# Layer 1's memory keys and values move into layer 0: projected during its attention, split into parts during its FFN

## The chip, the cores and the metric

The kernel runs on one core of a Trainium2 chip. The metric is device time in microseconds for one execution of the whole program. TensorE multiplies matrices into PSUM; VectorE and ScalarE work on SBUF and PSUM; GpSimd works on SBUF alone; the SyncE queue issues every load.

## The reference, cut to what matters

Two layers over 512 tokens of width 1024. Each layer normalises `x`, projects it, runs a token mixer on 12 heads (sparse attention with an index and a top-k in layer 0; compressed, selected and sliding-window attention in layer 1) beside a 4-head attention to a memory of 256 rows, projects all heads back and adds; then a SwiGLU FFN of width 2816 adds to `x`. The memory attention needs keys and values that depend on `mem`, on the layer's gain `mem_norm[i]` and on its weight alone, not on `x`:

```python
def memory_attention(q_mem, mem_n, w_kv_mem):          # mem_n = rmsnorm(mem, mem_norm[i])
    k, v = jnp.split(mem_n @ w_kv_mem, 2, axis=-1)     # 256 x 256 each
    s = jnp.einsum('bshd,bnhd->bhsn', q, k) * HEAD_DIM ** -0.5
    p = jax.nn.softmax(s, axis=-1)
    return jnp.einsum('bhsn,bnhd->bshd', p, v)
```

## The kernel before, in words

**Number format.** Every large product is made of three: an operand is cut into a high part of type fp32r and the rest, and `mm3` (lines 174 to 179) multiplies high by high, high by low and low by high. `weight` (line 159) loads a weight into one of four raw buffers (`wr`), ScalarE or VectorE casts the high part (`copy`, lines 148 and 150) and GpSimd or VectorE subtracts (lines 83 and 165). `raw` (line 168) loads into the same ring of four without cutting; it serves the memory projections, whose matmuls are plain fp32 and stand as two matmul instructions each in the trace.

**Stages.** `run` calls `setup`, `dsa` (layer 0's attention, 0 to 262 us of the profiled span), `ffn(0)` (to 610), `nsa` (layer 1's attention, to 916) and `ffn(1)`. An attention stage is a string of words, `SEQ[i]`, that `pipeline` turns into instructions in that order: `q:3` projects queries, `h:4` is the first half of a head unit (scores, exponentials, scaling of the rows), `H:4` the second (transposes on line 418, the cut of the weights on lines 422 to 427, weighted values on line 441), `m:0` and `M:0` the same for a pair of memory heads, `o:6` a part of the output projection, `t:128` so many steps of the top-k on VectorE (lines 686 to 692). The words give the priority; the framework's planner then writes a fixed order for each engine, in which an instruction may stand earlier than its word where the planner's own timeline has it ready.

**Memory.** `mem_stats` (word `ms`) makes the scale factors `mem_row` and `mem_col` once. `mem_kv(i)` (word `mkv`, in both strings) loads the memory again into four buffers of the tag `xs`, which also holds the 16 parts of the layer's normalised `x`, so that a buffer comes free when the last projection has read it. ScalarE multiplies eight pieces by the layer's gain (line 481); TensorE projects the keys (line 489), VectorE evicts them (line 491), and they are cut into a high and a low part, zero-padded by GpSimd (lines 494 to 498); TensorE projects the values (line 505) into two banks, and ScalarE and VectorE evict and cut them (lines 514 and 515). In layer 1 the word stands between `h:7` and `w:6`.

**PSUM.** Four tags share the eight banks: `mm`, `S` and `O` have two each, `T` four. Scores take `S` and `mm` in turn (`score_ps`).

Of the kernel before, what the change touches and what calls it, by code (L numbers as in the profile page):

```python
# [18 lines left out]
P = 128  # L19
# [10 lines left out]
OUT = -3e38  # L30
DOWN_SPLIT = (6, 5)
HALVED = 2
LAST = ("PPVP", "VVVV")
BUFS = {"xs": 17, "p": 10, "u": 8, "q": 12, "z": 2, "q1": 8, "qi": 4, "cy": 2, "k": 8, "m": 6, "r": 3, "t": 6, "o": 26, "o2": 6, "xg": 8}
RINGS = {"wr": 4, "wh": 3, "wl": 3}
STAY = {F32: 7 * KC + 2 + P + KC * S + S + P + NM + 1024 + 592 + RINGS["wr"] * KC * P, F32R: 4 * NB * P + 6 * P + (RINGS["wh"] + RINGS["wl"]) * KC * P}
BANKS = {"mm": 2, "S": 2, "T": 4, "O": 2}
FIRST = (0, 3)
IQ = False
# [6 lines left out]
CHUNKS = [((0, 1, 6, 7), (2, 3, 4, 5)), ((0, 1, 2), (6, 7, 3), (4, 5))]  # L46
TOPK = ((1, 2), (3,))
SEQ = ["""t:257 st iq:0 first iq:1 iq:2 iq:3 ix:1 ix:0 plan:1 ms ix:2 ix:3 kv mq:0 mq:1 q:2 q:0 q:3 t:128 h:4 q:1 h:0 q:4 q:5 mkv h:3 t:483 H:4 m:0
 m:1 h:1 h:5 M:0 M:1 h:2 H:3 h:6 t:5 H:2 h:9 H:6 H:5 H:9 h:8 h:7 H:0 plan:2 H:1 h:10 h:11 t:161 o:6 o:1 o:0 t:27 H:10 H:8 H:7 o:3 o:5 H:11
 o:7 o:4 o:2""",  # L50
       """plan:4 vc ks kc q:0 v ck kw h:0 plan:5 cv q:1 c:0 w:0 c:1 H:0 h:1 C:0 W:0 w:1 q:2 h:2 w:2 H:1 C:1 W:1 q:3 H:2 h:3 w:3 q:4 c:2 H:3 w:4 W:2
 w:5 W:3 C:2 h:4 c:3 q:5 h:5 H:5 mq:0 c:4 H:4 h:6 W:4 C:3 W:5 H:6 c:5 h:8 h:9 mq:1 h:7 mkv w:6 w:7 H:7 m:0 W:6 W:7 o:5 H:8 C:4 w:9 M:0 o:3
 o:2 m:1 o:1 h:10 o:0 H:9 o:6 W:9 w:8 w:10 M:1 o:7 o:4 W:8 C:5 h:11 H:10 o:12 o:11 w:11 H:11 W:10 o:13 W:11 o:9 o:14 o:8 o:10 o:15"""]
PLAN = [
    {"w": "V", "whi": "A", "stack": "P", "turn": "VP", "scale": "V", "shi": "A", "hhi": "VA", "hlo": "VP", "rmul": "VV", "radd": "V", "phi": "V", "plo": "V", "sqe": "PP", "irow": "VVPP", "sq": "PV"},
# [12 lines left out]
def r32(ap):  # L68
    return ap.bitcast(F32)
# [25 lines left out]
class Trunk:  # L95
# [378 lines left out]
    def mem_kv(self, i):  # L474
# [9 lines left out]
        for j in range(2):  # L484
# [12 lines left out]
                nc.scalar.copy(hi[h, sl], k[h])  # L497
                nc.vector.tensor_sub(lo[h, sl], k[h], r32(hi[h, sl]))
            keys.append((hi, lo))
        out = [self.ps(t)[:, :NM] for t in ("mm", "O")]  # L500
        for u in range(2):
            w = self.raw(io["wmv"][i, u])
            for b in range(2):
                for k in range(4):
                    nc.tensor.matmul(out[b], ms[4 * u + k][:, b * P : (b + 1) * P], w[:, k * NM : (k + 1) * NM], start=u + k == 0,
                                     stop=u == 1 and k == 3)
        vals = []
        for b in range(2):
            ps = out[b]
# [5 lines left out]
            nc.vector.scalar_tensor_tensor(dst[:, :, 64:], src, s, r32(dst[:, :, :64]), op0=ALU.mult, op1=ALU.subtract)  # L515
            vals.append(v)
        return keys, vals

    def mem_first(self, j, q, keys):

# [73 lines left out]
    def ffn(self, i):  # L594
        nc, io = self.nc, self.io
        xs, row = self.xs, None
        for half in range(2):
            acts = []
            for e in range(NFF // 2):
                j = half * (NFF // 2) + e  # L600
                g = self.proj(io["wf"][i, 2 * j], xs)
                u = self.proj(io["wf"][i, 2 * j + 1], xs, "S")
                if row is None:
                    row = self.stats()[1]
                a = self.slot("t", "fa")
                nc.vector.tensor_mul(a, g, row)  # L606
                nc.scalar.activation(a, a, AF.Silu)  # L607
                self.pool.tensor_mul(a, a, row)
                nc.vector.tensor_mul(a, a, u)  # L609
                hi, lo = self.pair("o", "f")  # L610
                nc.scalar.copy(hi, a)
                nc.vector.tensor_sub(lo, a, r32(hi))
                acts.append((hi, lo))
            for d in range(KC):
                if i and half and d == KC - HALVED:
                    self.down_last(acts)
                    break
                ps = self.ps("mm")
                k = 0
                for m in DOWN_SPLIT:  # L620
                    w = self.weight(io["wd"][i, half, d, :, k * P : (k + m) * P], m * P)
                    for e in range(m):
                        sl = slice(e * P, (e + 1) * P)
                        self.mm3(ps, (w[0][:, sl], w[1][:, sl]), acts[k], k == 0, k == NFF // 2 - 1)
                        k += 1
                nc.vector.tensor_add(self.x[d], self.x[d], ps)  # L626
                if half:
                    self.absorb(d, 1 if i == 0 else None)
                    if i:
                        self.last_gain(d, slice(0, S))  # L630
# [86 lines left out]
    def dsa(self):  # L717
# [75 lines left out]
        def query(j):  # L793
# [1 line left out]

        does = {"st": stats, "first": first, "iq": index_query, "ix": index, "ms": self.mem_stats, "kv": latent, "q": query,
                "mq": lambda j: self.mem_query(j, w, xs, row), "mkv": lambda: mkv.extend(self.mem_kv(0)), "t": self.tick,
                "o": lambda n: self.out_part(0, n % KC, CHUNKS[0][n // KC], "mm"), "plan": self.plan}
# [98 lines left out]
    def nsa(self):  # L897
# [31 lines left out]
        def comp_values():  # L929
# [2 lines left out]
        heads = [self.nsa_units(h, q, keys) for h in range(NH)]  # L932
        does = {"q": query, "mq": lambda j: self.mem_query(j, w, xs, row), "ks": lambda: key("ks"), "kw": lambda: key("kw"), "kc": lambda: unfold("kc"),
                "vc": lambda: unfold("vc"), "ck": comp_keys, "cv": comp_values, "v": lambda: self.values(col, xs),
                "mkv": lambda: mkv.extend(self.mem_kv(1)), "o": lambda n: self.out_part(1, n % KC, CHUNKS[1][n // KC], "mm"), "plan": self.plan}
# [232 lines left out]
```

## Time and profile before

| | |
|---|---|
| median of 3 runs | 1274.98 us (1273.6 to 1275.56) |
| the profiled execution | 1277.64 us, of which the span from first to last instruction is 1275.9 |
| TensorE matmul records, weight loads | 1234.9 us, 1026.0 us |
| VectorE, ScalarE, GpSimd | 622.1, 545.7, 798.4 us |
| mean granted TensorE clock | 0.980 of full |
| loaded from HBM | 105.25 MB |

A matmul's record is longer than the distance at which the next one can follow, so records overlap and a busy share near 100% may still hold idle time; the share of weight loads shows it better. Times of the trace are counted from the span's start. A row of the chain of waits says on which instruction, engine or transfer the last-ending chain of work stood, as a share of the stretch.

### The profile page before, as it was taken

The numbers are of one execution on the slowest core, as the hardware profiler recorded it, in microseconds if no ns is written. First come the engines' busy times: TensorE is split into PE (matmuls) and PEld (weight loads), VectorE is DVE, ScalarE is ACT, GpSimd is POOL, SyncE is SP. The second block draws the span as 40 slices with busy tenths as digits, with TensorE's granted clock in tenths as the row PEclk, the third lists the DMA queues.
The fourth block names the chain that finished last, engine by engine and source line by source line (L and its number), as shares of the span: only waits on it lengthen the run. The fifth ranks groups of instructions, "written<-read, shape, count | busy, mean of one in ns | idle before, by whom it ended". The sixth has DMA issues, their size and how long they took to land.

```text
span 1275.9 us, 17100 instructions
## 1 busy us (share of the span) xinstructions
PE 1234.9 (97%) x5882; PEld 1026.0 (80%) x5882; DVE 622.1 (49%) x1379; ACT 545.7 (43%) x1059; POOL 798.4 (63%) x1124
## 2 busy tenths in 40 slices
PE   7999889999999999999999999999999999999996
PEld 5888558888888888888888788887888888888886
DVE  6799976632221222234678998896521210111113
ACT  5535896433321223332247776785333322322231
POOL 9988884865543455447277674355986645667573
PEclk9999999999999999999986999999999999999998
DMA  7222002333223333223321101103232234333231
GB/s 267 89 74 89 11 1 76 99 99 99 89 78 100 118 95 99 81 89 116 107 99 50 36 15 57 32 32 118 78 96 96 85 88 114 111 97 91 69 91 66
DMA packets 40262, 108.44 MB, mean 85 GB/s; under 512 B 4720, under 2 KB 10480, under 8 KB 40176
## 3 DMA queue, kind: packets, MB, share of 16 engines
q1 hardware_dynamic: 40176, 107.36, 27.2%
q8 instruction: 46, 0.75, 0.3%
q14 instruction: 40, 0.33, 0.1%
HBM read 105.25 MB, written 2.10 MB: 84 GB/s over the span
## 4 chain that ended last, share of the span: by engine, by line
PE 77%; DVE 14%; ACT 3%; POOL 2%; DMA 2%; issue 1%; SPq 0%; DVEq 0%; ACTq 0%; POOLq 0%
PE ps L179 23%; PE ps L178 23%; PE ps L177 23%; PE ps L441 3%; PE ps L418 2%; DVE sc L690 2%; DVE stay L689 2%; DVE p L385 1%; DVE ul L427 1%; DMA mem<-in_memT 1%; POOL sq L83 1%; PE ps L380 1%; ACT p L391 1%; PE ps L381 1%; POOL stay L83 1%
## 5 line engine op out<-in xcount | busy, mean ns | idle before, releaser
L83 POOL TENSOR_TENSOR stay<-stay,stay 128x256 fp32r<-128x256 f32 (+1 forms) x601 | 441.5, 764 | 306.7 <-ACT stay L150 166.0
L150 ACT CAST stay<-stay 128x1024 fp32r<-128x1024 f32 (+4 forms) x208 | 189.4, 911 | 518.6 <-PE ps L178 455.3
L177 PE MATMUL ps<-xh,stay 128*128 128x512 f32 x912 | 358.9, 394 | 6.8 <-ACT xh L238 6.5
L179 PE MATMUL ps<-xh,stay 128*128 128x512 f32 x912 | 359.1, 394 | 1.2 <-DVE stay L165 1.2
L178 PE MATMUL ps<-xl,stay 128*128 128x512 f32 x912 | 358.0, 393 | 0.5 <-DVE xl L239 0.5
L177 PEld LDWEIGHTS ps<-xh,stay 128*128 128x128 f32 x912 | 173.4, 190 | 43.1 <-ACT xh L238 6.5
L179 PEld LDWEIGHTS ps<-xh,stay 128*128 128x128 f32 x912 | 173.0, 190 | 37.6 <-DVE stay L165 1.5
L178 PEld LDWEIGHTS ps<-xl,stay 128*128 128x128 f32 x912 | 172.9, 190 | 37.0 <-DVE xl L239 1.0
L178 PE MATMUL ps<-fl,stay 128*128 128x512 f32 (+1 forms) x352 | 134.8, 383 | 0.0
L179 PE MATMUL ps<-fh,stay 128*128 128x512 f32 (+1 forms) x352 | 134.6, 382 | 0.0
L177 PE MATMUL ps<-fh,stay 128*128 128x512 f32 (+1 forms) x352 | 134.6, 382 | 0.0
L609 DVE TENSOR_TENSOR fa<-fa,ps 128x512 f32<-128x512 f32 x44 | 30.2, 687 | 183.5 <-PE ps L179 166.1
L626 DVE TENSOR_TENSOR stay<-stay,ps 128x512 f32<-128x512 f32 x30 | 20.7, 689 | 155.6 <-PE ps L179 155.6
L606 DVE TENSOR_TENSOR fa<-ps,row 128x512 f32<-128x512 f32 x44 | 30.2, 690 | 128.2 <-PE ps L179 116.5
L391 ACT ACTIVATE p<-p,stay 128x384 f32<-128x384 f32 (+3 forms) x144 | 80.2, 559 | 18.0 <-DVE stay L385 17.4
L83 POOL TENSOR_TENSOR fa<-fa,row 128x256 f32<-128x256 f32 x88 | 65.3, 764 | 24.9 <-ACT fa L607 24.9
L177 PEld LDWEIGHTS ps<-fh,stay 128*128 128x128 f32 x352 | 66.1, 188 | 12.9
L178 PEld LDWEIGHTS ps<-fl,stay 128*128 128x128 f32 x352 | 66.1, 188 | 12.9
L179 PEld LDWEIGHTS ps<-fh,stay 128*128 128x128 f32 x352 | 66.2, 188 | 12.8
L83 POOL TENSOR_TENSOR p<-p,stay 128x128 f32<-128x128 f32 (+1 forms) x106 | 56.1, 557 | 32.4 <-DVE stay L401 21.7
L427 DVE TENSOR_TENSOR ul<-ps,uh 128x512 fp32r<-128x512 f32 (+1 forms) x103 | 62.7, 619 | 7.1 <-ACT uh L426 5.3
L418 PE MATMUL ps<-stay,p 128*128 128x128 f32 x360 | 55.8, 278 | 5.1 <-POOL p L83 2.1
(273 smaller groups left out, 2018.2 us busy)
## 6 DMA issues: line engine op xcount, KB each, us to landing
stay<-in_wf SPq DMA_DIRECT2D x88, 512.0 KB, 3.6
stay<-in_w SPq DMA_DIRECT2D x26, 512.0 KB, 3.5
stay<-in_wd SPq DMA_DIRECT2D x32, 384.0 KB, 3.1
stay<-in_wd SPq DMA_DIRECT2D x32, 320.0 KB, 2.9
mem<-in_memT SPq DMA_DIRECT2D x12, 256.0 KB, 3.8
stay<-in_wo SPq DMA_DIRECT2D x6, 512.0 KB, 3.5
stay<-in_wo SPq DMA_DIRECT2D x16, 192.0 KB, 2.4
stay<-in_xT SPq DMA_DIRECT2D x8, 256.0 KB, 6.7
```

The lines of the kernel that those rows point to most:

```text
L83: op(out[:, sl], x[:, sl], y[:, sl])
L150: self.nc.scalar.copy(out, x)
L177: mm(out, lhs[0], rhs[0], start=start, stop=False)
L178: mm(out, lhs[0], rhs[1], start=False, stop=False)
L179: mm(out, lhs[1], rhs[0], start=False, stop=stop)
L391: self.nc.scalar.activation(p, p, AF.Exp, scale=-1.0, bias=least, accum_out=total)
L418: nc.tensor.transpose(ps[:, off : off + P], ap, self.ident)
L427: nc.vector.tensor_sub(lo, ps[:, :w], r32(hi))
L441: self.nc.tensor.matmul(out, v if len(parts) > 1 else r32(v), t, start=start and i == 0, stop=stop and i == len(parts) - 1)
L606: nc.vector.tensor_mul(a, g, row)
L609: nc.vector.tensor_mul(a, a, u)
L689: nc.vector.max(m8, s)
```

## The change: what it does

`mem_kv` is no longer called for layer 1. Three new functions take its place. `next_keys(j)`, words `xk:0` and `xk:1` in layer 0's string, loads the memory (the first time), multiplies it by layer 1's gain, projects one of the two key tiles into a bank of tag `S` and evicts it, scaled, to a buffer of its own. `next_values`, word `xv`, projects both value tiles into one bank of tag `S` and evicts them through ScalarE. `next_parts` cuts the four tiles and is called in `ffn(0)` ahead of the second half. Four such buffers of 256 columns are added to the constant area. In `mem_kv`, which now serves layer 0 alone, the values go to the two halves of one `mm` bank, one output after the other, with both weights loaded ahead.

```diff
- ... h:1 h:5 M:0 M:1 h:2 H:3 h:6 t:5 H:2 h:9 H:6 H:5 H:9 h:8 ...            (SEQ[0])
+ ... h:1 h:5 M:0 M:1 xk:0 h:2 H:3 h:6 xk:1 t:5 H:2 h:9 H:6 H:5 xv H:9 h:8 ...
- ... h:8 h:9 mq:1 h:7 mkv w:6 w:7 H:7 m:0 ...                               (SEQ[1])
+ ... h:8 h:9 mq:1 h:7 w:6 w:7 H:7 m:0 ...
     def mem_kv(self, i):
...
-        out = [self.ps(t)[:, :NM] for t in ("mm", "O")]
-        for u in range(2):
-            w = self.raw(io["wmv"][i, u])
-            for b in range(2):
-                for k in range(4):
-                    nc.tensor.matmul(out[b], ms[4 * u + k][:, b * P : (b + 1) * P], w[:, k * NM : (k + 1) * NM], ...)
+        bank, ws = self.ps("mm"), [self.raw(io["wmv"][i, u]) for u in range(2)]
+        out = [bank[:, b * NM : (b + 1) * NM] for b in range(2)]
+        for b in range(2):
+            for k in range(KC):
+                nc.tensor.matmul(out[b], ms[k][:, b * P : (b + 1) * P], ws[k // 4][:, k % 4 * NM : (k % 4 + 1) * NM], ...)
+    def next_keys(self, j):
+        nc = self.nc
+        if j == 0:
+            self.next_mem, self.next_k, self.next_v = [], [self.c([P, NM], name="nk") ...], [self.c([P, NM], name="nv") ...]
+            for c, m in enumerate(self.load_mem("xs")):
+                for e in range(2):
+                    ...
+                    nc.scalar.activation(m[:, sl], m[:, sl], AF.Copy, scale=self.gains[:, g : g + 1])
+                    self.next_mem.append(m[:, sl])
+        ps, w = self.ps(NEXT[0])[:, :NM], self.raw(self.io["wmk"][1, j])          # NEXT = ("S", "S")
+        for k in range(KC):
+            nc.tensor.matmul(ps, w[:, k * P : (k + 1) * P], self.next_mem[k], start=k == 0, stop=k == KC - 1)
+        nc.vector.scalar_tensor_tensor(self.next_k[j], ps, -0.125, self.mem_row, op0=ALU.mult, op1=ALU.mult)
+    def next_values(self):
+        ... as the new lines of mem_kv, into self.ps(NEXT[1]), with layer 1's weights and self.next_mem
+        for b in range(2):
+            nc.scalar.activation(self.next_v[b], out[b], AF.Copy, scale=self.mem_col[:, b : b + 1])
+    def next_parts(self):
+        for k in self.next_k:
+            hi, lo = self.slot("m", "mkh", F32R), self.slot("m", "mkl", F32R)
+            for t in (hi, lo):
+                nc.gpsimd.memset(r32(t[:64, NM:]), 0.0)
+                nc.gpsimd.memset(r32(t[64:, :NM]), 0.0)
+            for h, sl in ((slice(0, 64), slice(0, NM)), (slice(64, P), slice(NM, S))):
+                nc.scalar.copy(hi[h, sl], k[h])
+                nc.vector.tensor_sub(lo[h, sl], k[h], r32(hi[h, sl]))
+        for v in self.next_v:
+            ...
+            nc.scalar.copy(dst[:, :, :64], src)
+            nc.vector.tensor_sub(dst[:, :, 64:], src, r32(dst[:, :, :64]))
     def ffn(self, i):
         for half in range(2):
+            if i == 0 and half == 1:
+                self.next_parts()
     def nsa(self):
-        mkv, z, keys = [], {}, {}
+        mkv, z, keys = self.next_kv, {}, {}
```

## Rows read from the trace of the kernel before

**Rows 1.** The page's engine line: busy us, share of the span, instructions.
```profile
PE 1234.9 (97%) x5882; PEld 1026.0 (80%) x5882; DVE 622.1 (49%) x1379; ACT 545.7 (43%) x1059; POOL 798.4 (63%) x1124
```

**Rows 2.** Layer 0's FFN, second half: the chain by line, then the busy-time window.
```profile
by line: PE ps L178 33.4%; PE ps L179 33.3%; PE ps L177 33.3%; PE ssq L201 0.1%
...
430.00:610.00 180.00, 180.00 (x798) 149.09 (x797) 55.42 (x68) 52.73 (x68) 94.42 (x125) 1.00 0.32 97
```

**Rows 3.** Windows, layer 1: busy PE, PEld, DVE, ACT, POOL; clock, DMA share, GB/s.
```profile
770.00:780.00 10.00, 10.00 (x60) 8.72 (x60) 9.88 (x34) 9.47 (x28) 2.87 (x4) 1.00 0.25 80
780.00:790.00 10.00, 10.00 (x49) 8.72 (x48) 7.45 (x17) 5.23 (x13) 7.44 (x12) 1.00 0.08 23
790.00:800.00 10.00, 10.00 (x56) 8.94 (x55) 6.26 (x22) 5.96 (x17) 3.51 (x6) 1.00 0.33 97
800.00:810.00 10.00, 9.44 (x53) 7.38 (x53) 8.44 (x22) 8.46 (x31) 1.86 (x4) 1.00 0.08 20
810.00:820.00 10.00, 9.42 (x59) 8.01 (x58) 9.94 (x23) 7.70 (x20) 3.23 (x6) 1.00 0.07 22
```

**Rows 4.** The chain of waits by line, 774 to 800 us.
```profile
by line: PE ps L489 26.8%; PE ps L505 16.7%; DMA stay<-in_wo 8.7%; PE ps L381 7.8%; PE ps L380 7.8%; PE ps L177 7.1%; PE ps L179 7.1%; PE ps L178 7.0%; PE ps L441 3.8%; DVE p L385 2.6%; ACT stay L150 2.0%; DVE mv L515 1.9%; ACT mv L514 1.5%
```

**Rows 5.** Windows as in rows 3, layer 0's attention; the last is solid TensorE.
```profile
130.00:150.00 20.00, 17.17 (x76) 11.55 (x75) 19.70 (x58) 14.89 (x56) 19.49 (x39) 0.91 0.05 14
150.00:165.00 15.00, 13.14 (x61) 8.39 (x58) 12.97 (x45) 14.76 (x41) 10.31 (x20) 1.00 0.00 0
165.00:180.00 15.00, 12.35 (x64) 8.32 (x65) 10.16 (x33) 13.80 (x36) 13.06 (x24) 1.00 0.01 2
180.00:195.00 15.00, 12.60 (x49) 8.79 (x48) 9.92 (x23) 11.32 (x29) 8.70 (x15) 0.89 0.00 1
...
210.00:236.00 26.00, 26.00 (x126) 21.64 (x125) 13.99 (x24) 13.36 (x23) 12.09 (x15) 1.00 0.31 102
```

**Rows 6.** The chain by line, 130 to 165 us and 165 to 195 us.
```profile
by line: DVE sc L690 17.0%; DVE stay L689 15.8%; DVE p L385 13.7%; DVE stay L528 12.9%; ACT p L391 11.8%; DVE ul L427 5.4%; issue 3.8%; DVE ho L450 3.7%; ACT ho L449 3.3%; ACT oh L150 3.2%; ACT uf L422 2.9%; DVE stay L397 2.6%; DVE ho L838 
...
by line: PE ps L441 26.6%; PE ps L418 15.7%; ACT ho L837 9.4%; ACT p L391 8.1%; ACT uh L426 5.8%; PE ps L177 4.4%; ACT p L411 4.4%; PE ps L380 4.1%; PE ps L381 4.1%; ACT uf L422 4.0%; ACT o L150 3.4%; PE ps L179 3.0%; PE ps L178 3.0%; issue
```

**Rows 7.** Matmuls that read the memory, 690 to 810: duration, first and last start.
```profile
L489 PE MATMUL ps<-mem,stay x32: 378/379/431, 782.1 to 791.2; 128*128 128x256 f32 x32
L505 PE MATMUL ps<-stay,mem x32: 377/379/382, 783.0 to 797.8; 128*128 128x256 f32 x32
```

**Rows 8.** Timeline of TensorE: a run of twenty.
```profile
787.12 4.48 PE L489 MATMUL ps<-mem,stay 128*128 128x256 f32 x20
```

**Rows 9.** Window 774 to 805, lines 498, 515, 491, 497, 514 in turn: busy, count.
```profile
774.00:805.00 31.00, 2.16 (x4) 1.00 0.24 71
...
774.00:805.00 31.00, 0.96 (x2) 1.00 0.24 71
...
774.00:805.00 31.00, 0.85 (x2) 1.00 0.24 71
...
774.00:805.00 31.00, 1.61 (x4) 1.00 0.24 71
...
774.00:805.00 31.00, 0.95 (x2) 1.00 0.24 71
```

**Rows 10.** Line 481: durations, its waits, a run; then one of the memsets.
```profile
L481 ACT ACTIVATE mem<-mem,stay x16: 492/496/512, 24.0 to 782.8; 128x256 f32<-128x256 f32 x16
...
  DMA mem<-in_memT: 3.5, 3
...
109.03 1.71 ACT L481 ACTIVATE mem<-mem,stay 128x256 f32<-128x256 f32 x4 [1.80 <-DMA mem<-in_memT]
...
L494 POOL MEMSET mkh<- x4: 303/304/304, 0.9 to 135.2; 64x256 f32 x4
```

**Rows 11.** The load queue: wo in layer 1; what it waited for, 130 to 260.
```profile
784.72 15.90 SPq L163 DMA_DIRECT2D stay<-in_wo  x7
...
SPq L163 <- ACT stay L150: 83.6, 8, 62.0
```

More of the change, by code (lines that the diff above doesn't have):

```diff
@@ L32 @@
 HALVED = 2
+NEXT = ("S", "S")
 LAST = ("PPVP", "VVVV")
@@ L35 @@
 RINGS = {"wr": 4, "wh": 3, "wl": 3}
[L36 removed]
+STAY = {F32: 7 * KC + 2 + P + KC * S + S + P + NM + 1024 + 592 + 4 * NM + RINGS["wr"] * KC * P, F32R: 4 * NB * P + 6 * P + (RINGS["wh"] + RINGS["wl"]) * KC * P}
 BANKS = {"mm": 2, "S": 2, "T": 4, "O": 2}
@@ L499, in mem_kv @@
             keys.append((hi, lo))
-        out = [self.ps(t)[:, :NM] for t in ("mm", "O")]
-        for u in range(2):
-            w = self.raw(io["wmv"][i, u])
-            for b in range(2):
-                for k in range(4):
-                    nc.tensor.matmul(out[b], ms[4 * u + k][:, b * P : (b + 1) * P], w[:, k * NM : (k + 1) * NM], start=u + k == 0,
-                                     stop=u == 1 and k == 3)
+        bank, ws = self.ps("mm"), [self.raw(io["wmv"][i, u]) for u in range(2)]
+        out = [bank[:, b * NM : (b + 1) * NM] for b in range(2)]
+        for b in range(2):
+            for k in range(KC):
+                nc.tensor.matmul(out[b], ms[k][:, b * P : (b + 1) * P], ws[k // 4][:, k % 4 * NM : (k % 4 + 1) * NM], start=k == 0, stop=k == KC - 1)
         vals = []
@@ L517, in mem_kv @@
         return keys, vals
+    def next_keys(self, j):
+        nc = self.nc
+        if j == 0:
+            self.next_mem, self.next_k, self.next_v = [], [self.c([P, NM], name="nk") for _ in range(2)], [self.c([P, NM], name="nv") for _ in range(2)]
+            for c, m in enumerate(self.load_mem("xs")):
+                for e in range(2):
+                    sl = slice(e * NM, (e + 1) * NM)
+                    g = 3 * KC + 2 * c + e
+                    nc.scalar.activation(m[:, sl], m[:, sl], AF.Copy, scale=self.gains[:, g : g + 1])
[4 more added lines that the diff above has]
+        nc.vector.scalar_tensor_tensor(self.next_k[j], ps, -0.125, self.mem_row, op0=ALU.mult, op1=ALU.mult)
@@ new lines, in next_values @@
+    def next_values(self):
+        nc = self.nc
+        bank, ws = self.ps(NEXT[1]), [self.raw(self.io["wmv"][1, u]) for u in range(2)]
+        out = [bank[:, b * NM : (b + 1) * NM] for b in range(2)]
+        for b in range(2):
+            for k in range(KC):
+                nc.tensor.matmul(out[b], self.next_mem[k][:, b * P : (b + 1) * P], ws[k // 4][:, k % 4 * NM : (k % 4 + 1) * NM], start=k == 0, stop=k == KC - 1)
+        for b in range(2):
+            nc.scalar.activation(self.next_v[b], out[b], AF.Copy, scale=self.mem_col[:, b : b + 1])
@@ new lines, in next_parts @@
+    def next_parts(self):
+        nc, keys, vals = self.nc, [], []
+        for k in self.next_k:
[6 more added lines that the diff above has]
+                nc.vector.tensor_sub(lo[h, sl], k[h], r32(hi[h, sl]))
+            keys.append((hi, lo))
+        for v in self.next_v:
+            t = self.slot("m", "mv", F32R)
+            src, dst = v.rearrange("p (h d) -> p h d", h=4), t.rearrange("p (h d) -> p h d", h=4)
+            nc.scalar.copy(dst[:, :, :64], src)
+            nc.vector.tensor_sub(dst[:, :, 64:], src, r32(dst[:, :, :64]))
+            vals.append(t)
+        self.next_kv = keys, vals
```

8 lines of the change are left out of this document (4 added, 4 removed).

## The prediction

> **What bounds the kernel now.** I read the page's engine line first: TensorE 97% busy, the other engines 43 to 63% [rows 1]. A busy record of TensorE is longer than the pitch at which its matmuls follow each other, so 97% hides idle time; I therefore go stage by stage, by ten-microsecond windows and by the chain of waits. Layer 0's FFN is TensorE alone: its chain is the three lines of the split product, a third each, while VectorE has 55.4 of 180 us to do and GpSimd 94.4 [rows 2]. The two attention stages are not like that, and the change lives in them.
>
> Layer 1, around the block that is taken out: the reader sees VectorE at 9.88 of 10 us just before it, at 7.45 and 6.26 in the two windows of 780 to 800, and at 8.44 and 9.94 after, while TensorE is full throughout [rows 3]. The chain of 774 to 800 names the cause: 43.5% of it is lines 489 and 505, the memory projections, and another 8.7% a wait for a weight of the output projection [rows 4]. So VectorE, else the bound there, starves for these 20 us while TensorE projects memory.
>
> Layer 0, 130 to 195 us: VectorE has 19.70 of 20 us to do until 150, ScalarE 14.76 of 15 and 13.80 of 15 until 180; weight loads, which take 21.64 of 26 us where TensorE is full, take 37.05 of these 65 [rows 5]. At the full stretch's share (0.832) these are 44.5 us of solid TensorE, so about 20.5 us of it are free, an estimate. The chain goes over VectorE's top-k lines and ScalarE's exponentials first and is 61% TensorE's from 165 to 195 (lines 441, 418, 177, 380, 381, 179, 178) [rows 6].
>
> **Layer 1: what goes.** 64 matmul instructions of 128x256 (32 on line 489, 32 on line 505) [rows 7]; twenty in a row take 4.48 us, so the pitch is (4.48 - 0.38) / 19 = 0.216 us [rows 8], and all take 13.8 us. VectorE loses 2.16 + 0.96 + 0.85 = 3.97 us, ScalarE 1.61 + 0.95 in the same stretch [rows 9] and eight scalings of 0.496 us each [rows 10]. What is left of 780 to 800 is 20 - 13.8 = 6.2 us on TensorE and 13.71 - 3.97 = 9.74 on VectorE; ScalarE's list is shorter than that, GpSimd's is as long but has idle time on both sides [rows 3]. So VectorE is late next. At the neighbours' mean load (9.88, 8.44 and 9.94 of 10, that is 0.942) its 9.74 us take 10.3, and the gain is 9.7 us. The ends: 4.0 us, if VectorE stays the bound without a break so that only its own share is won; and 14.5 us, the chain's part that the block causes (26 us times 0.435, 0.087 and the 0.034 of lines 514 and 515) [rows 4]. A loss there is excluded: every engine's list only gets shorter and the rest of the order string is unchanged. I take 9.7, since VectorE is the nearer limit in the rows.
>
> In the queue of the loads, two of wmv leave the ring of four raw buffers, so the seven loads of wo that now start only at 784.72 [rows 11] can come sooner; the 8.7% of the chain that waits for one, 2.26 us, belongs to the upper end, not to the 9.7.
>
> **Layer 0: what is added.** The same 64 matmuls, 13.8 us, against the 20.5 us free: I cost them at nothing; without that cover, at TensorE's 61% of the chain from 165 to 195, 13.8 x 0.61 = 8.4 us. ScalarE gets eight scalings, in a row 1.71 / 4 = 0.43 us each [rows 10], and two evictions of values at about 0.47 (half of line 514's 0.95): 4.3 us. It has 10.2 us idle from 130 to 195, 5.1 of them before 150 where VectorE is the bound, nearly none from 150 to 165 [rows 5]. The scalings need only the landed memory and can lie early, the evictions cannot: I cost half, 2.15 us (ends 0 and 4.3). VectorE gets two evictions of keys, half of 0.85 us each; half of that on the chain, 0.4 (ends 0 and 0.85). Sum 2.5 us.
>
> Below nothing: the granted clock is 0.91 of full in 130 to 150 and 0.89 in 180 to 195 [rows 5], so TensorE ran some 3.5 us at its lower level, 1.2 GHz, in each, after thin stretches. Matmuls that fill these could keep it at 2.4 GHz; in 180 to 195, where TensorE is on the chain, that gives back 15 x 0.11 = 1.65 us. The ends of layer 0 are thus -1.65 and 4.3 + 0.85 + 8.4 = 13.5. The Trainium skill, "TensorE: Matmul & The Clock Gate", section "What's actually happening", has the gate follow how busy TensorE has recently been; by it the sum would be better by those 1.65 us. I leave it in the range, since the rows do not show that the dips lie where the new matmuls fall.
>
> The loads are four of memory, two of wmk and two of wmv. They enter the queue ahead of the first wo loads and take the four raw buffers, so each of those wo loads waits until its predecessor's matmuls have read. In this stage the queue stood idle behind full buffers for up to 62.0 us at a time [rows 11]; I cost it at nothing, and at one landing like that one, 2.26 us, if the values' projection runs so late that the output projection at 190 has no weight.
>
> **FFN and the small edits.** The splitting put ahead of layer 0's second FFN half costs VectorE 2.16 + 0.96, ScalarE 1.61 + 0.95 and GpSimd eight memsets of 0.30 us [rows 9, 10]; the stage's chain is TensorE's alone and hides all of it [rows 2]. If that cover were gone it would be VectorE's 3.1 us. Layer 0's own values now go to one bank, output by output: same matmuls, and at worst its two evictions one after the other, 0.95 us; I take 0.
>
> **Sum.** -9.7 + 2.5 = -7.2 us. The profiled execution took 1277.64 us, which gives 1270.4; it lies 2.66 above the median of the runs, 1274.98, and against that the forecast is 1267.8 us.
>
> **Rivals.** *The moved matmuls meet a TensorE that is on the chain.* Place: layer 0 from 165 on. Its matmuls run in the order written at build time; if the projections of xk:1 and xv stand ahead of the heads' transposes and weighted products, they delay these by 8.4 us; if they slip behind 195, where TensorE is full, by the whole 13.8. With the 2.5 of the other engines that is 10.9 to 16.3 against a gain of 9.7: 1.2 to 6.6 slower, 1279 us in the middle. It decides from the point at which more than about half of the 13.8 us is on the chain (7.2 us). For it: the order string puts all three behind the memory heads, and 165 to 195 is 61% TensorE's. Against: in layer 1 the lines 489 and 505 lie interleaved rather than in one block (the second starts at 783.0, the first's last at 791.2) [rows 7], so such matmuls can fill holes, and 20.5 us are free. *VectorE does not let go.* Layer 1 gives only its 4.0 us, layer 0 takes 2.5: -1.5, or 1273.5 us. For it: 9.88 and 9.94 of 10 on either side; against: 6.3 us of idle VectorE inside the block. *Everything fits.* The chain's 14.5 us go, layer 0 takes 1: 1261.5 us. For it: the wo loads come sooner; against: VectorE's 9.74 us have to be done somewhere. *ScalarE waits at the head of its queue.* ScalarE stood idle 3.5 us in three waits of line 481 for the memory's landing [rows 10]; if the new scalings come to its head before their loads have landed, the exponentials behind them wait as long: -7.2 + 3.5 = -3.7, or 1271.3 us. Against: the loads can be issued long before 150, and only one of the waits shown is as long as 1.80. The Trainium skill, "TensorE: Matmul & The Clock Gate", section "Architectural detail", says that ScalarE's queue is strictly first in, first out; by that rule nothing overtakes the scalings, and the trace's waits agree.
>
> **Chances.** Forecast 0.52 (own range 1264 to 1271), everything fits 0.14, VectorE 0.16, ScalarE's queue 0.06, TensorE on the chain 0.12. A measurement of this kernel can tell about 0.2%, 2.5 us, from no change. Faster: the first two, most of ScalarE's queue (0.05) and a little of VectorE's (0.03): 0.74. The same: most of VectorE's and small parts of others, 0.13. Slower: the TensorE rival and the worse side of VectorE's, 0.13. The range 1261 to 1278 leaves out half of the two outer cases.
>
> **What would show it.** Right: in layer 1's attention no matmul of a memory projection, VectorE above 9 of 10 us through the former block, and the stage from 610 to 916 shorter by 8 to 11 us; in layer 0 the 64 matmuls between 125 and 195 with TensorE's weight loads up from 37 us and layer 0's FFN starting 1 to 4 us later; the FFN as long as before. Wrong: a later FFN start by more than 7 us, idle VectorE where the block was, or the projections behind 195.

## The result and the profile after

The changed kernel takes 1288.97 us (median of 4 runs, 1287.87 to 1290.33), the kernel before 1275.27 us beside it (1273.6 to 1276.11): a ratio of 1.0107, 95% interval 1.0095 to 1.0118. It is 13.7 us slower; 7.2 us faster was forecast.

The profiled execution's span is 1288.6 us against 1275.9. Cut where TensorE starts the first product of the next stage's input, the spans fall into these parts (us; read from the traces; these cuts lie earlier than the rough bounds of 262 and 916 us named ahead of the prediction; the kernels after the first two are experiments below):

```
                       layer 0's    layer 0's   layer 1's    layer 1's
                       attention    FFN         attention    FFN
before                   247.2        362.0       288.0        378.7
after                    263.7        361.9       284.7        378.2
l1_only                  244.1        362.0       280.2        378.7
l0_only                  253.6        362.0       290.8        378.4
first_key_on_gpsimd      256.9        361.9       280.7        378.4
before_3T                247.5        363.6       295.8        378.7
after_3T                 259.9        363.6       282.8        378.8
cut_in_ffn_3T            250.5        362.0       284.7        378.4
```

A row is one execution, and a part of it can differ by some 3 us without any edit: l1_only's layer 0 has the written order of before on TensorE, VectorE and ScalarE and is 3.1 us shorter. In its first 50 us TensorE had its full clock, in before it was granted 0.93, in the changed kernel 0.93 too, in *l0_only* and *first_key_on_gpsimd* 1.00.

So, at the same clock at the start, layer 0's attention took 16.5 us more than before, layer 1's 3.3 less, the FFNs the same. Line numbers are from here on those of the kernel that a row comes from; the changed kernel's are higher than before's by 1 up to line 500 and by 45 to 47 behind the new functions. First the engine line of the changed kernel, which answers to [rows 1], and its chain by line in the second half of layer 0's FFN with the window, which answer to [rows 2]:

```profile
PE 1240.3 (96%) x5882; PEld 1031.5 (80%) x5882; DVE 634.1 (49%) x1379; ACT 546.2 (42%) x1061; POOL 797.0 (62%) x1124
...
by line: PE ps L180 33.4%; PE ps L179 33.4%; PE ps L178 33.3%
...
446.00:626.00 180.00, 180.00 (x796) 149.06 (x795) 55.11 (x67) 53.17 (x68) 94.54 (x125) 1.00 0.32 97
```

VectorE has 12.0 us more to do over the whole span, for work that was only moved, and no more of it in the FFN (55.11 against 55.42), where the cut was to stand. The cut's four subtractions for the keys are line 554 (the two for the values, line 560, start at 185.9 and 186.5 us); the trace has them here (line, count, shortest/median/longest ns, first and last start), after them the projections:

```profile
L554 DVE TENSOR_TENSOR mkl<-stay,mkh x4: 422/1655/6294, 145.9 to 174.8; 64x256 fp32r<-64x256 f32 x4
...
L531 PE MATMUL ps<-mem,stay x32: 377/379/796, 138.9 to 170.0; 128*128 128x256 f32 x32
...
L540 PE MATMUL ps<-stay,mem x32: 378/379/382, 174.8 to 183.5; 128*128 128x256 f32 x32
```

All four stand in layer 0's attention, between 145.9 and 174.8 us: the cut hangs only on the projected tiles, and the planner drew it forward from the FFN, where the program's text has it, into the attention. One of the four took 6294 ns instead of the 0.54 us that such a subtraction took in layer 1 before (2.16 us for four) [rows 9]. The timelines of VectorE and of GpSimd around it:

```profile
145.92 6.29 DVE L554 TENSOR_TENSOR mkl<-stay,mkh 64x256 fp32r<-64x256 f32 x1 [0.66 <-ACT mkh L553]
152.14 0.68 DVE L736 MAX8 stay<-sc 128x8 f32<-128x512 f32 x1
```

```profile
145.57 0.72 POOL L81 TENSOR_TENSOR o<-ho,o 128x256 fp32r<-128x256 f32 x1
146.26 2.89 POOL L84 TENSOR_TENSOR mp<-mp,stay 128x256 f32<-128x256 f32 x5
149.11 1.40 POOL L84 TENSOR_TENSOR stay<-stay,stay 128x256 fp32r<-128x256 f32 x2
150.47 1.46 POOL L84 TENSOR_TENSOR p<-p,stay 128x128 f32<-128x128 f32 x4
```

GpSimd works without a gap; the 12 instructions shown run from 145.57 to 151.93. VectorE's subtraction, which reads two tiles in SBUF, starts 0.35 us into the first of them and ends at 152.21, just after the last is over. Behind it VectorE's pass over the scores (line 386) is late, ScalarE's exponentials (line 392) wait 5.9 us for that, and TensorE's transposes (line 419) as long. These are TensorE's two longest waits from 120 to 215 us (total, times, longest); the second ends at 204.7 and is another one, for a cast in ScalarE's queue:

```profile
PE ps L419 <- DVE stay L386: 5.9, 1, 5.9
PE ps L178 <- ACT o L151: 3.1, 1, 3.1
```

The windows of layer 0's attention (columns as in [rows 3]) answer to [rows 5]: in 150 to 165 TensorE is busy 9.88 of 15 us and was 13.14, ScalarE 7.83 and was 14.76, and TensorE's granted clock is 0.77 there, where it was full before; in 195 to 210 it is 0.78. TensorE so loses the wait, and then runs part of the stretch behind it at 1.2 GHz.

```profile
130.00:150.00 20.00, 16.30 (x71) 11.72 (x71) 18.47 (x41) 14.44 (x55) 15.10 (x30) 0.91 0.04 14
150.00:165.00 15.00, 9.88 (x39) 6.23 (x40) 12.85 (x37) 7.83 (x20) 6.53 (x13) 0.77 0.05 17
165.00:180.00 15.00, 15.00 (x77) 12.39 (x76) 14.00 (x35) 12.42 (x36) 10.67 (x20) 1.00 0.12 36
180.00:195.00 15.00, 15.00 (x75) 11.28 (x74) 9.42 (x26) 13.61 (x35) 8.70 (x15) 1.00 0.15 54
195.00:210.00 15.00, 11.44 (x44) 8.72 (x44) 9.97 (x27) 12.02 (x31) 10.93 (x21) 0.78 0.00 1
```

The chain by line, 120 to 215 us, answers to [rows 6]. VectorE's top-k (lines 736 and 737) has 4.3% and 3.1% of it, where it had 8.6% and 9.3% in the same stretch of before, and the two moved projections stand in it with 7.3% each, 13.9 of 95 us. Before, then after:

```profile
by line: PE ps L441 12.3%; PE ps L418 9.6%; DVE sc L690 9.3%; DVE stay L689 8.6%; ACT p L391 6.9%; DVE p L385 6.1%; PE ps L177 5.7%; PE ps L179 5.0%; PE ps L178 5.0%; DVE stay L528 4.7%; ACT ho L837 3.0%; ACT uf L422 2.3%; DVE mkl L498 2.2%
...
by line: PE ps L442 14.8%; PE ps L419 10.9%; issue 8.8%; PE ps L531 7.3%; PE ps L540 7.3%; ACT p L392 6.1%; DVE stay L736 4.3%; ACT mp L576 4.1%; DVE sc L737 3.1%; DVE p L386 2.8%; DVE mkl L499 2.7%; ACT ho L884 2.7%; DMA stay<-in_wo 2.7%; 
```

In layer 1, where the block was, VectorE is now busy 12.51 of 14 us (8.9 of 10), against 7.45 and 6.26 of 10 [rows 3], so that the idle VectorE is gone nearly as forecast (above 9 of 10):

```profile
783.00:797.00 14.00, 13.05 (x93) 11.69 (x92) 12.51 (x39) 11.63 (x33) 5.19 (x9) 1.00 0.00 1
```

### The profile page after: what moved, and what is told of

The parts are those of the page before. It is cut to its first block, busy times and chain, and to the rows that moved or that the text cites. A ratio compares the mean times of both kernels' runs of the same rounds, so it can differ in the third digit from the quotient of the medians.

```text
span 1288.6 us, 17111 instructions
## 1 busy us (share of the span) xinstructions
PE 1240.3 (96%) x5882; PEld 1031.5 (80%) x5882; DVE 634.1 (49%) x1379; ACT 546.2 (42%) x1061; POOL 797.0 (62%) x1124
## 4 chain that ended last, share of the span: by engine, by line
PE 77%; DVE 12%; POOL 4%; ACT 3%; issue 2%; DMA 1%; DVEq 0%; SPq 0%; ACTq 0%; POOLq 0%
PE ps L180 23%; PE ps L179 22%; PE ps L178 22%; PE ps L442 3%; PE ps L419 2%; POOL sq L84 2%; DVE sc L737 2%; DVE p L386 2%; DVE stay L736 1%; DVE ul L428 1%; POOL stay L84 1%; PE ps L381 1%; DVE p L410 1%; PE ps L382 1%; ACT p L392 1%
## 5 line engine op out<-in xcount | busy, mean ns | idle before, releaser
L427 ACT CAST uh<-ps 128x512 fp32r<-128x512 f32 (+1 forms) x103 | 53.2, 534 | 17.8 <-PE ps L419 14.9
```

The lines of the kernel that those rows point to most:

```text
L427: nc.scalar.copy(hi, ps[:, :w])
```

## The experiments

The order of every engine is written by the planner, so an edit moves other instructions too. Each experiment is therefore compared with the kernel that differs from it by the one edit; times are medians, ratios are to the kernel before with a 95% interval.

**The two halves apart.** *l1_only* is the kernel before without layer 1's memory keys and values (layer 1 uses layer 0's, so its output is another); *l0_only* is the changed kernel whose layer 1 makes its own again as before, the early ones being made and left unused.

```diff
- mkv, z, keys = [], {}, {}                  # l1_only; and "mkv" out of SEQ[1]
+ mkv, z, keys = self.first_kv, {}, {}       # what mem_kv(0) made
- ... mq:1 h:7 w:6 w:7 ...                   # l0_only
+ ... mq:1 h:7 mkv w:6 w:7 ...               # with mkv.extend(self.mem_kv(1))
```

> Before, with layer 1's memory projection and cut taken out and nothing put in its place: layer 1's memory heads read layer 0's keys and values (that part of the computation is left out). If the forecast's step for layer 1 is right, the time falls by about 9.7 us (1265.5). The changed kernel's layer 1 only gained 3.3 us, having lost 6 us between 700 and 777 before it won 9.2 at the former block. If that loss belongs to the removal, this run gains about 3 us (1272); if it belongs to what is added in layer 0, this run gains 9 to 10.

> The changed kernel, with layer 1 projecting and cutting its own memory as before, so that the work put into layer 0 is done and not used. If the two layers add up, layer 0's cost of 16.5 us stands alone: 1291 to 1292 us, and layer 1 is as long as before (288.0 us). If part of the cost came from layer 1's shorter string, it is less than 1289.

l1_only: 1267.38 us, 0.9945 [0.993, 0.996], 8.2 us faster than the 1275.53 beside it. l0_only: 1288.11 us, 1.0111 [1.0091, 1.0131], 12.6 slower than the same. The removal is worth nearly what was forecast; the loss is layer 0's. But the halves do not add up: 12.6 - 8.2 is 4.4 us slower, the whole change 13.7, and l0_only lies under the 1291 to 1292 expected of halves that do.

A piece is missing in l0_only. Its layer 0 has the changed kernel's written order (but for eight memsets on GpSimd), so the two profiled executions can be laid side by side. l0_only's (the fastest of its runs, 1286.59) spent 253.6 us there, not 263.7: none of its four subtractions took over 1.09 us, though the first also begins just behind the start of a GpSimd instruction. That subtraction and GpSimd beside it in l0_only, then the transposes of TensorE behind it in l0_only and in the changed kernel, then the first 50 us of both in that order:

```profile
143.34 0.69 DVE L554 TENSOR_TENSOR mkl<-stay,mkh 64x256 fp32r<-64x256 f32 x1 [0.78 <-ACT mkh L553]
143.03 0.73 POOL L81 TENSOR_TENSOR o<-ho,o 128x256 fp32r<-128x256 f32 x1
143.71 3.26 POOL L84 TENSOR_TENSOR mp<-mp,stay 128x256 f32<-128x256 f32 x5
...
146.31 0.41 PE L419 MATMUL ps<-stay,mp 128*128 128x128 f32 x2 [0.56 <-DVE stay L386]
154.22 0.66 PE L419 MATMUL ps<-stay,mp 128*128 128x128 f32 x2 [5.89 <-DVE stay L386]
...
0.00:50.00 50.00, 41.46 (x185) 32.93 (x186) 36.74 (x65) 25.20 (x37) 47.61 (x67) 1.00 0.61 208
0.00:50.00 50.00, 41.42 (x176) 33.34 (x177) 35.41 (x61) 25.20 (x37) 48.14 (x68) 0.93 0.62 210
```

The changed kernel is 2.6 us behind when its subtraction starts (145.92 against 143.34), its clock having been 0.93 in the first 50 us; 7.9 behind at these transposes; and 10.1 behind at the start of the FFN, after a clock of 0.77 in 150 to 165, where l0_only was granted 1.00. So the long wait, with the lower clock right behind it, cost layer 0 7.5 us.

**The small edits.** *bank_only* is the kernel before with the values in one bank (those of both layers, as `mem_kv` still serves both there); *early_S_mm* is the changed kernel with the three words behind `mkv`, and the early values in an `mm` bank.

```diff
- out = [self.ps(t)[:, :NM] for t in ("mm", "O")]                        # bank_only
+ bank, ws = self.ps("mm"), [self.raw(io["wmv"][i, u]) for u in range(2)]
- ... mkv h:3 t:483 H:4 ... M:1 xk:0 h:2 H:3 h:6 xk:1 t:5 ... xv H:9     # early_S_mm
+ ... mkv xk:0 xk:1 xv h:3 t:483 H:4 ... M:1 h:2 H:3 h:6 t:5 ... H:9
```

> Before, with only the edit of layer 0's own memory values (one bank, one output after the other, both weights loaded ahead). The forecast had 0 us for it, at worst 0.95. The order of layer 0's instructions comes out differently in some hundred places, so the rival is that the new order, not the added work, costs several us of the 16.5: then 1279 or more. By the forecast 1274 to 1276.

> The changed kernel with the three words moved up to stand right behind layer 0's own projection of the memory (values into a bank of tag mm), so that the 64 matmuls run before 135 us, where VectorE's top-k sets the pace, and the cut still runs in the attention. If the moved matmuls cost their time because they stand on the chain between 139 and 185 (13.9 us of the chain there), the time falls by 6 us or more (under 1283). If the cost is the cut that waits behind GpSimd and the evictions, it falls by less than 3 us (1286 to 1289).

bank_only: 1273.04 us, 0.9988 [0.9978, 0.9997], a little under what was expected; the bank edit is no part of the loss. early_S_mm: 1285.83 us, 1.009 [1.0075, 1.0105], 3.1 us under the changed kernel, between its two expectations; its layer 0 took 257.0 us without a long subtraction (longest 0.73 us), its layer 1's attention 286.7.

**The cut put where the text has it.** That order needs one PSUM bank more, so the base is the kernel with 3 banks of `T`.

```diff
- BANKS = {"mm": 2, "S": 2, "T": 4, "O": 2}                              # all four
+ BANKS = {"mm": 2, "S": 2, "T": 3, "O": 2}
-                 self.next_parts()                                      # the last two
+                 with self.tc.issue_after(after[0].ins), self.tc.issue_after(after[1].ins):
+                     self.next_parts()      # after = the last cast and subtraction of the first FFN half
```

> The kernel before with the PSUM pool T cut from 4 banks to 3, nothing else: the base for the next three kernels, which need the bank. Both theories: 1275 to 1283 us; if the fourth T bank is worth much more than that (over 8 us), the three kernels on this base say less about the change itself.

> The changed kernel with 3 T banks. Theory A (the cut, which the written order drew forward into layer 0's attention, holds VectorE and GpSimd up there: 6 to 8 us) and theory B (the 64 matmuls of 13.8 us lie on TensorE's chain in layer 0, the cut costs under 2) both expect what the change did with 4 banks: 12 to 15 us over the kernel before with 3 banks. Layer 0's attention ends 9 to 17 us later, layer 1's is 3 to 8 us shorter.

> The changed kernel with 3 T banks, with the cut of the keys and values held behind the first half of layer 0's FFN, where the text of the kernel puts it. Theory A: 6 to 8 us under the changed kernel with 3 banks, all of it won in layer 0's attention, and the FFN no longer. Theory B: within 2 us of it.

> As the last one, and the projections of layer 1's memory keys and values stand in the unit of layer 0's own, right behind them, instead of in three later units. Theory A: another 2 to 4 us less (what the same move gave with the cut left in attention), so 8 to 12 under the changed kernel with 3 banks. Theory B: the matmuls cost where they stand on the chain; in the unit of layer 0's own, which is TensorE-bound, up to 14 us, so equal to the last one or up to 4 above.

before_3T 1287.18 us; after_3T 1281.98 (1277.87 to 1286.74); cut_in_ffn_3T 1276.3 (1274.97 to 1277.36), 1.0007 [0.9997, 1.0016] to the kernel before; together_cut_in_ffn_3T 1283.66. The fourth `T` bank is worth 11.9 us to the kernel before, more than the 8 that were to warn, so no sum is carried from this base to the other.

Both theories missed on after_3T: it was to be 12 to 15 us over before_3T and is 5.2 under it, and cut_in_ffn_3T is 10.9 under. On this base the change pays. In the profiles layer 1's attention, the stage that the projections left, took 295.8 us in before_3T (288.0 with 4 banks) and 282.8 and 284.7 in the two; layer 0's took 247.5, and 259.9 and 250.5.

Within the base, the cut's place is worth 5.7 us by the medians, just short of theory A's 6 to 8. In the FFN the four subtractions take 0.42 us each and the stage is as long as before (362.0):

```profile
L554 DVE TENSOR_TENSOR mkl<-stay,mkh x4: 411/421/422, 375.4 to 376.7; 64x256 fp32r<-64x256 f32 x4
```

after_3T's profiled execution, the longest of its five (1286.74), has one of 6.46 us:

```profile
144.46 6.46 DVE L554 TENSOR_TENSOR mkl<-stay,mkh 64x256 fp32r<-64x256 f32 x1 [1.35 <-ACT mkh L553]
144.26 0.73 POOL L81 TENSOR_TENSOR o<-ho,o 128x256 fp32r<-128x256 f32 x1
```

The last kernel met neither theory: the projections put together behind layer 0's own cost 7.4 us more than spread out, where A expected a gain and B at most 4 more. So where on TensorE they stand has a price, which speaks for B, beside A.

**The same with 4 T banks.** With the early keys in `T` and the values in `O` both orders fit (banks_TO_cut_in_ffn has the edit with `issue_after` from above as well).

```diff
- NEXT = ("S", "S")                                                      # all three
+ NEXT = ("T", "O")
- nc.vector.tensor_sub(lo[h, sl], k[h], r32(hi[h, sl]))                  # banks_TO_cut_on_gpsimd; the values' too
+ nc.gpsimd.tensor_sub(lo[h, sl], k[h], r32(hi[h, sl]))
```

> The changed kernel with 4 T banks as it was, its early key projections in a T bank and the value projection in an O bank instead of both in S. The cut still stands in layer 0's attention. Base of the next two. Theory A (the cut in attention costs 6 to 8 us) and theory B (the matmuls cost it) both: within 5 us of the changed kernel, 1284 to 1294 us.

> As banks_TO, with the cut held behind the 11th activation of layer 0's FFN's first half; the order of TensorE and GpSimd is otherwise that of banks_TO. Theory A: 6 to 10 us under banks_TO, layer 0's attention not over 4 us longer than in the kernel before, and layer 1's 8 to 11 us shorter, so 1267 to 1272 us if the banks cost nothing. Theory B: within 2 us of banks_TO.

> As banks_TO, with the 6 subtractions of the cut on GpSimd instead of VectorE; the casts stay on ScalarE, all of it still in layer 0's attention. If the loss is VectorE's, standing in its subtractions until GpSimd is done (theory A1): 3 to 7 us under banks_TO, the VectorE no longer having one of them at 2 us or more. If the loss is ScalarE's casts and the order written around them (theory A2): within 2 us of banks_TO, or slower, since GpSimd takes 4 to 5 us more of work in its full stretch. Theory B: within 2 us.

1279.16, 1278.38 and 1280.57 us: all the same within their spread, and banks_TO missed its 1284 to 1294. On these banks theory A is wrong. There is also no long subtraction to save: in banks_TO the first stands at 164.4, 18 us later, and the longest of the keys' takes 0.87 us. Yet layer 0 takes 259.6 us (258.2 with the cut in the FFN): 11 to 12 us over before, for which the cut is not to blame.

**Loads or matmuls.** Two edits on each base: the weights of the early projections in tiles of their own instead of the raw ring that also feeds `wo`; and 56 of the 64 matmul records left out.

```diff
- ps, w = self.ps(NEXT[0])[:, :NM], self.raw(self.io["wmk"][1, j])       # own_buffers; the values' too
+ ps, w = self.ps(NEXT[0])[:, :NM], self.held(self.io["wmk"], j)         # two tiles of the tag "xg"
- for k in range(KC):                                                    # few_matmuls; the values' too
+ for k in range(1):
```

> As banks_TO_cut_in_ffn, with the four weights of the early projections loaded into tiles of their own, ahead of the memory, instead of into the ring of four raw buffers that feeds wo. Theory W (the wo loads wait behind the projections for a raw buffer, ScalarE stands at their cast and TensorE behind it): 3 to 6 us under banks_TO_cut_in_ffn, the wait of 2.8 us for wo in layer 0's chain gone. Theory M (the matmuls are on TensorE's chain): within 1.5 us of it.

> The same edit on cut_in_ffn_3T. Theory W: 1 to 3 us under it (its ScalarE waited 2.1 us for wo). Theory M: within 1 us.

> As banks_TO, with 56 of the 64 matmul records of the early projections left out (the first of each group stays, so layer 1's memory keys and values are wrong); loads, evictions and the cut stay. Theory M: 8 to 12 us under banks_TO (56 by 0.216 us are 12.1), all in layer 0's attention. Theory W: within 3 us, as the weights hold the raw buffers as long.

> The same matmuls left out of cut_in_ffn_3T, whose layer 0's attention is only 3 us longer than before's. Theory M in its mild form (what the matmuls cost is what layer 0 grew): 2 to 4 us under it. In its strong form (12 us of chain): 8 to 12 under it. Theory W: within 2 us.

Own buffers: 1278.26 against 1278.38, and 1277.2 against 1276.3. Theory W falls, although the wait that it names did go. The longest waits of the load queue, 100 to 260 us, of banks_TO_cut_in_ffn and then of banks_TO_own_buffers:

```profile
SPq L164 <- PE ps L531: 42.7, 2, 36.4
```

```profile
SPq L164 <- ACT stay L151: 94.4, 9, 72.4
```

In the first the queue waits up to 36.4 us for the early projections to give their buffers back; in the second its longest wait is for ScalarE, behind full buffers, as in before [rows 11]. Loads that come sooner bought nothing.

Few matmuls: 1271.12 us on the T and O banks, 8.0 under banks_TO for 56 x 0.216 = 12.1 us left out, and its layer 0 is 8.0 us shorter (251.6). In the chain of 120 to 215 us of banks_TO the two projections stand with 12.6%; without them the top-k and the pass over the scores on VectorE come back to its head:

```profile
by line: PE ps L442 10.6%; PE ps L531 8.0%; ACT p L392 5.9%; DVE p L386 5.8%; PE ps L419 5.1%; PE ps L540 4.6%; DVE stay L736 4.3%; POOL mp L84 4.2%; DVE sc L737 3.8%; ACT uf L423 3.5%; ACT ho L884 3.2%; PE ps L178 3.1%; DVE mkl L499 2.9%; 
```

```profile
by line: DVE p L386 11.6%; DVE sc L737 9.8%; DVE stay L736 8.5%; PE ps L442 7.8%; PE ps L419 6.7%; POOL p L84 4.6%; DVE stay L573 4.6%; PE ps L179 4.4%; PE ps L178 4.1%; PE ps L180 4.1%; DVE ul L428 3.9%; DVE mkl L554 3.8%; issue 3.6%; DVE 
```

On the 3-bank base the same cut bought nothing: 1277.72 against 1276.3, where 2 to 4 less were expected. In the profiles its layer 0 is 4.8 us shorter, but the FFN 1.6 and layer 1 1.5 us longer, in a written order that differs in some 80 places on TensorE (that of the other pair in some 90). So the matmuls have a price of 8.0 us on the T and O banks, and none that shows on this base.

**The changed kernel itself.** These three keep its banks (`S`, `S`, 4 of `T`) and, but for a few places, its written order of layer 1.

```diff
-         for k in range(KC):            # few_value_matmuls: range(1) in next_values
+         for k in range(4):             # half_key_matmuls, in next_keys
- nc.vector.tensor_sub(lo[h, sl], k[h], r32(hi[h, sl]))                  # first_key_on_gpsimd
+ (nc.gpsimd if self.next_k[0] is k else nc.vector).tensor_sub(lo[h, sl], k[h], r32(hi[h, sl]))
```

> The changed kernel with 28 of the 32 records of the early value projection left out (layer 1's memory values are wrong); the keys, the loads, the evictions and the cut stay, and layer 1's order is the changed kernel's. Theory M (the matmuls lie on TensorE's chain here too): 28 by 0.215 are 6.0, so 4 to 6 us under the changed kernel's 1289, 1283 to 1285. Theory S (layer 0's loss is VectorE standing in the cut's subtractions, with what follows): within 2 us of it, 1287 to 1291, with a subtraction over 5 us in the profile again.

> The changed kernel with 16 of the 32 records of the early key projections left out (layer 1's memory keys are wrong), all else as it was. Theory M: 16 by 0.215 are 3.4, 2 to 4 us under the changed kernel. Theory S: the first key tile is cut some 2 us earlier beside another piece of GpSimd's work; the time follows what the longest subtraction is: about 6 us under the changed kernel if none is over 1 us, no change if one is at 5 or more.

> The changed kernel with the two subtractions of its first key tile on GpSimd instead of VectorE; the other four stay on VectorE, every matmul stays, and layer 1's order is the changed kernel's. Theory S (VectorE stood in the first of them for 6.3 us, and the two groups of runs lie 11.8 us apart by it): no subtraction of the cut over 2.5 us on VectorE, all runs in one group at 1276 to 1281, 8 to 12 us under the changed kernel. Theory M (the matmuls): within 3 us of 1289, since all 64 stay.

few_value_matmuls met neither theory as written: its 12 runs fall in two groups, seven at 1274.23 to 1279.75 and five at 1287.04 to 1289.99, with medians of 1276.87 and 1288.05, 11.2 us apart. The profiled one is of the upper group and has the long subtraction, and layer 0's written order is the changed kernel's up to it:

```profile
L554 DVE TENSOR_TENSOR mkl<-stay,mkh x4: 423/1659/6254, 146.0 to 174.9; 64x256 fp32r<-64x256 f32 x4
```

That the lower group has none is inferred: no execution of it was profiled. half_key_matmuls: 1275.41 us (1272.6 to 1279.73), one group, 13.6 under the changed kernel for 3.5 us of matmuls. Its longest subtraction takes 1.45 us, but another operation of VectorE there, of only 128x4, stands for 4.57 us, from 145.31 to 149.88; GpSimd's run ends at 148.44 + 1.41 = 149.85:

```profile
145.31 4.57 DVE L398 TENSOR_SCALAR stay<-stay 128x4 f32<-128x4 f32 x1
```

```profile
144.90 0.74 POOL L81 TENSOR_TENSOR o<-ho,o 128x256 fp32r<-128x256 f32 x1
145.59 2.90 POOL L84 TENSOR_TENSOR mp<-mp,stay 128x256 f32<-128x256 f32 x5
148.44 1.41 POOL L84 TENSOR_TENSOR stay<-stay,stay 128x256 fp32r<-128x256 f32 x2
```

So a wait of this kind has no price by its length alone: this one did not keep the kernel from 1275.

first_key_on_gpsimd leaves nothing out: 1278.35 us (12 runs, 1275.39 to 1280.84), 1.002 [1.0009, 1.0032], 10.6 us under the changed kernel, as theory S expected. Two subtractions of 0.64 us are the whole edit, but the planner wrote layer 0 anew behind them (TensorE's order differs in some 30 places, from 147 us on), and the 10.6 us hold that too:

```profile
L554 POOL TENSOR_TENSOR mkl<-stay,mkh x2: 637/639/641, 149.0 to 151.2; 64x256 fp32r<-64x256 f32 x2
L554 DVE TENSOR_TENSOR mkl<-stay,mkh x2: 511/760/1008, 162.4 to 164.1; 64x256 fp32r<-64x256 f32 x2
```

It keeps both early projections in `S` and comes out where banks_TO does (1279.16), so the choice of banks as such is not the price. The value matmuls are cheap on these banks: the 28 left out, 6.0 us of TensorE, put few_value_matmuls' upper group 0.9 us under the changed kernel and its lower group 1.5 under first_key_on_gpsimd.

Of the kernels that compute all and have the early projections, none beat the kernel before; cut_in_ffn_3T equals it.

## Why the prediction was wrong

**Layer 1's gain was right.** 9.7 us were forecast. Alone it measured 8.2 us (l1_only), and in the profiles layer 1's attention became 7.8 shorter there, 7.3 in first_key_on_gpsimd. VectorE was next, at 12.51 of 14 us. In the changed kernel's own profile only 3.3 us arrived; the other 4.0 to first_key_on_gpsimd, which has the same written order in layer 1 but for a few places, were lost ahead of the block and behind it, in stretches at a lower clock (last section).

**The step that failed first: "the stage's chain is TensorE's alone and hides all of it".** The FFN does hide the cut (cut_in_ffn_3T: 362.0 us). But the cut was not in the FFN. The text that stands ahead of the prediction says that an instruction may stand earlier than its word; I applied that to no step. In layer 0's attention one subtraction met a run of GpSimd and held VectorE for 6.29 us, in its fullest stretch. Price: 7.5 us in layer 0, by l0_only's profile in the same written order; by whole times 10.6 (first_key_on_gpsimd, with its other order in layer 0) and 11.2 (the two groups of few_value_matmuls, if the wait is what parts them). In the profiles 6.8 of the 10.6 lie in layer 0, the clock of its first 50 us included, and 4.0 in layer 1 at its lower clock; that the wait causes the latter is not shown. The trace of before had a case of the wait, which I did not look for: six subtractions of one form, five at about 0.69 us and one at 3.27, beside GpSimd at its back-to-back work.

```profile
886.65 3.27 DVE L452 TENSOR_TENSOR ol<-ho,oh 64x512 fp32r<-64x512 f32 x1 [0.76 <-ACT oh L150]
```

```profile
884.50 6.00 POOL L83 TENSOR_TENSOR stay<-stay,stay 128x256 fp32r<-128x256 f32 x8
```

The Trainium skill, "SBUF — State Buffer", section "Who interferes with whom", says that a VectorE instruction with two inputs in SBUF contends with a GpSimd instruction that reads SBUF. The trace agrees (6.29 us against 0.42), and shows besides that the wait can last through a whole run of GpSimd's instructions, 12 here, not through one. It need not: the one in before ended at 889.92, ahead of the run's end at 890.50.

**The second: "the same 64 matmuls, 13.8 us, against the 20.5 us free: I cost them at nothing".** Without the long wait first_key_on_gpsimd is still 2.7 us over before, although layer 1 gives some 8.2 (l1_only): layer 0 cost some 10.9 us there, not 2.5. On the T and O banks, where layer 0 cost 12.0 by the same count, the matmuls made 8.0 of it (of 12.1 left out), close to the 8.4 that the prediction had without cover, and 4.0 were left for all else. The free time was counted as a sum over 65 us, but it lay in holes that TensorE had because it waited for VectorE and ScalarE; a block of sixteen matmuls (3.5 us, and 5.2 at 138.86, where part of it ran at the lower clock) put into the order ahead of what those engines wait for delays them, and the holes come again later. That mechanism is argued from the chains, not shown apart. The rival of the moved matmuls, 1279 us, had it; I gave it 0.12. That first_key_on_gpsimd takes 1278.35 is no proof of it: on these banks the price of all 64 was not measured, the value matmuls showed next to none, and on the 3-bank base none showed.

One reading against this rival was wrong. Lines 489 and 505 were said to lie interleaved rather than in one block, so that such matmuls can fill holes. They are interleaved with each other: 48 of the 64 stand in 10.5 us of a full TensorE, among four others. All of line 489 and 505, then all of TensorE (columns as in [rows 3], the first with TensorE alone):

```profile
782.10:792.60 10.50, 10.45 (x48) 1.00 0.20 58
...
782.10:792.60 10.50, 10.50 (x52) 9.24 (x51) 5.81 (x13) 3.67 (x10) 5.96 (x10) 1.00 0.20 58
```

**Right:** the FFN's length, the bank edit (no loss), the loads (the `wo` wait of 2 to 3 us is there and its removal moved nothing). **Sum of what was measured:** -8.2 from layer 1, 10.9 in layer 0 without the long wait, 10.6 with it: 13.3 of the 13.7. This is bookkeeping and no check, since the last two terms are differences to first_key_on_gpsimd. It says how the loss divides: at most half of layer 0's is the long wait, and of the rest the part that the matmuls have is measured on other banks only.

**What stays open.** Why kernels with both projections in `S` meet the long wait in some executions, and the profiled ones with `T` and `O` in none, is not shown beyond this: with `T` and `O` the first subtraction stands 18 us later. l0_only takes 1286.59 to 1292.23 us though its one profile has no long wait; its TensorE stood 3.1 us at line 178 for a cast in ScalarE's queue, as the changed kernel's did, and that was not tried apart. early_S_mm is like it in having no long wait at 1285.83, and half_key_matmuls had a wait of 4.57 us at no price. What the moved matmuls cost on the changed kernel's own banks is open as well.

## What to carry to other kernels

Work that hangs only on early data can be drawn forward by a planner: find out where a moved instruction will stand in each engine's order, not where the text has it, before you name what hides it. Idle time of an engine that waits for others is not free room: blocks put there delay what the others wait for, so a first estimate of their price is that engine's share of the chain (here 8.4 us, where 8.0 were measured on one set of banks and none on another). Where VectorE and GpSimd are both near full, look at the longest of each form's durations, not its mean.

## What the runs showed of the hardware that was not expected

Which engine stands is not told by the offset of the starts. 0.31 us into the same GpSimd instruction (line 81) the subtraction took 0.69 us in l0_only, and GpSimd's next five took 3.26 us instead of 2.89; 0.35 us into it, in the changed kernel, it took 6.29, and 0.20 us into it, in after_3T, 6.46. The same order of instructions so gave both. few_value_matmuls, one program, has two groups of times 11.2 us apart; that this is what parts them is likely, not shown.

TensorE's clock in layer 1's thin stretch, 60 to 80 us after its start, differs between kernels with nearly the same order there. The windows of before, and of half_key_matmuls:

```profile
669.20:689.20 20.00, 17.64 (x83) 15.87 (x83) 14.68 (x34) 14.48 (x33) 16.04 (x22) 0.56 0.23 75
```

```profile
680.50:700.50 20.00, 15.95 (x90) 13.83 (x90) 17.14 (x48) 16.06 (x42) 16.99 (x23) 0.83 0.20 63
```

At 0.56 TensorE spent most of the window at 1.2 GHz and issued 83 matmuls, at 0.83 it issued 90. half_key_matmuls' layer 1 took 277.7 us; the changed kernel's, with the same order but for a few places, 284.7, at 0.56 there and at 0.93 and 0.91 in the two windows behind it, where half_key_matmuls was granted 1.00. Why it falls into one or the other was not found; the 7.0 us are as much as the whole change was to bring.
